# Eight weight buffers filled ahead of the ids' loads, and another order of the experts

## The chip, the cores and the metric

The kernel runs on one core of a Trainium2 chip. The metric is the time of one execution on the device, in microseconds, median of several runs. The core has TensorE (matmuls and transposes), VectorE, ScalarE, GpSimd (POOL), the queue engine SyncE (SP), and 16 DMA engines that all queues share.

## The reference

One encoder layer over 1536 tokens (a sequence of 1024 and one of 512) of width 1024, in fp32. A first half mixes tokens: a projection, a pooled part and differential attention, then an output projection and a residual. The second half is a mixture of experts, and the change lies there:

```python
pg = jax.nn.softmax((xt @ w_rg) + b_rg); g_top, g_idx = lax.top_k(pg, 1)      # 1 of 4 groups
...
e_top, e_loc = lax.top_k(pe, TOP_K)                                          # 2 of its 8 experts
...
hid = jax.nn.silu(xblk @ w_gate[e]) * (xblk @ w_up[e])                       # 1024 -> 512
return hid @ w_down[e]                                                       # 512 -> 1024
```

Each of the 32 experts has three matrices of 2 MB, 6 MB together. The layer's output is the residual plus the gated sum of two experts per token, and a last RMSNorm.

## The kernel before

Up to about 692 us of the span run projection, attention, output projection and routing. Then comes the expert stage, then a closing stage from about 1376 us that adds the last experts' rows, normalises and stores.

**Routing.** `route` finds for each token its two experts and writes token and gate into a table in memory with indirect DMAs from GpSimd (L945), one region per expert. `schedule` ranks experts 2 to 31 by their number of tokens while the first expert runs, and writes the ranking to `K["order"]`. Experts 0 and 1 (`STATIC`) are not ranked; they come first.

**Order and capacity.** `slots()` gives the sequence of positions: experts 0 and 1 as ranks 30 and 31, then the ranks in the order of the constant `ORDER`; rank 0 is the expert with the most tokens. `CAPS` gives each rank its capacity, the number of rows that are computed for it: 252, 252, 208, 200, 192, 160, 160, 160, 128, ... down to 32, and 148 and 48 for experts 0 and 1. A capacity is cut into blocks of up to 128 rows. At a capacity of 64 or less the expert is "whole": its weights are used raw, in fp32 matmuls (L1071 for w_gate and w_up, L1083 for w_down). Above that the weights are split into a high and a low part, high by ScalarE (L104), low by VectorE (L108), and a full block takes three matmuls per weight tile (L112 to L114); a block of up to 64 rows beside a full one takes two (L1113, L1114).

**The order of the work.** TensorE, VectorE, ScalarE and SP run in the written order. At position i TensorE does w_gate of i, w_up of i, then w_down of i-1. In between come transposes of the rows of i+1 and of the hidden values of i-1 (L1129), whose results ScalarE and VectorE take out of PSUM (L1138, L1139). GpSimd gathers the rows of i+2 (L1149) and adds results of i-1 to memory (L1204). SP loads the ids, which the gathers and the scatters need, four positions ahead (L1064).

**Weights.** A matrix is loaded in two pieces of 1 MB (`fetch`, L1047), numbered in the order of use: pieces 0 and 1 are w_gate of position 0, 2 and 3 w_up of 0, 4 and 5 w_gate of 1, 6 and 7 w_up of 1, 8 and 9 w_down of 0, and so on. There are `RAW` = 8 buffers, so piece k+8 waits until piece k has been split, or, for a whole expert, until its matmuls have read it. Each piece has two halves, the unit of splitting; splits are issued `AHEAD` = 7 halves ahead of the matmuls, and the split halves have `CUT` = 8 buffers.

**The start.** Pieces 0 and 1 are loaded during attention. `fetch(SOON)` loads the pieces below number SOON on SP as soon as the right-hand memory is free; behind it on SP stand the ids' loads of positions 0 and 1, which wait until routing has written the table. During the first block of expert 0 (64 rows that were known early) no further pieces are fetched. Then the pieces up to number 9 are fetched from ScalarE's queue, and from there on the splits issue them on SP:

```python
        at = [0, 0, 0, SOON]
...
        fetch(SOON)
...
        for i in range(STATIC):
            ids(i)
            gather(i)
...
        at[3] = len(stream) + 2
...
        fetch(6 * STATIC - 2, nc.scalar)
        ids(2)
```

Of the kernel before, what the change touches and what calls it, by code (L numbers as in the profile page):

```python
# [32 lines left out]
STATIC = 2  # L33
RAW, CUT = 8, 8
AHEAD = 7
SOON = 6
FIRST = 2
FINAL = (2,) * 6
LAST = (2, 3, 4, 3)
# [6 lines left out]
PACE = (3, 1, 1, 1, 1, 1, 1, 0)  # L46
WHOLE = 64
DELAY = dict(out=1, hidden=1, silu=1, evac=1, turn_h=2, turn_x=4, end_h=3, stack=3)
ORDER = (0, 17, 18, 13, 1, 19, 20, 14, 2, 21, 22, 8, 3, 23, 24, 15, 4, 27, 9, 5, 26, 16, 6, 25, 10, 12, 7, 11, 29, 28)
CAPS = (252, 252, 208, 200, 192, 160, 160, 160, 128, 112, 108, 100, 96, 88, 80, 76, 72, 64, 64, 60, 60, 56, 56, 52, 48, 36) + (32,) * 4 + (148, 48)  # L50
VORDER = tuple(range(8, 12)) + tuple(range(8))
TGORDER = (2, 0, 1)
# [1165 lines left out]
def slots():  # L1218

    return [(NE - STATIC + e, e) for e in range(STATIC)] + [(j, None) for j in ORDER]  # L1220

# [67 lines left out]
def experts(tc, A, S, K, RO, outs):  # L1289
    nc = tc.nc  # L1290
    E = Experts(tc, A, S, K)
    with ExitStack() as ctx:
# [47 lines left out]
        raws, pieces = {}, {}  # L1340
        at = [0, 0, 0, SOON]

# [21 lines left out]
        def fetch(k, queue=None):  # L1364
            while len(stream) <= at[0] < k:
                tail_step(at[0] - len(stream))
                at[0] += 1
            while at[0] < min(k, len(stream)):
                name, i, h = stream[at[0]]
                raws[at[0]] = E.fetch(name, expert(i), h, queue)  # L1370
                at[0] += 1
# [50 lines left out]
        E.open_weights(ctx, RAW - FIRST, CUT, side="right")  # L1422
        fetch(SOON)
        for _ in rest:
# [159 lines left out]
```

## Time and profile before

| | us |
|---|---|
| median of 3 runs | 1425.19 |
| lowest and highest | 1423.98, 1440.15 |
| profiled execution | 1428.79 |
| its span, first to last instruction | 1426.9 |
| TensorE busy in the span | 1312.8 |
| VectorE busy | 810.1 |
| ScalarE busy | 658.3 |

All times in the rows are microseconds from the start of the span. The granted clock of TensorE is a share of 2.4 GHz; it has two levels, 1.2 and 2.4 GHz. The DMA share is the mean busy share of the 16 DMA engines; in a short window it can be a little over 1, since a packet counts where it starts.

### The profile page before, as it was taken

The page shows a single profiled execution, that of the slowest core. Times are in us where ns is not written, and L with a number is a line of the kernel's source. Part 1 is how long each engine was busy: PE and PEld are TensorE (multiplying, and loading weights), DVE is VectorE, ACT ScalarE, POOL GpSimd, SP SyncE. Part 2 cuts the span into 40 slices and gives each one's busy share as a digit, 9 for nine tenths or more (in the row PEclk, how much of TensorE's full clock was granted, in tenths as well). Part 3 has the DMA queues.
Part 4 walks back from the last instruction along what each step waited for, and adds up shares of the span by engine and source line. Part 5 has one row for each costly group of instructions (what it writes and reads, how often), then busy time and mean ns, then how long its engine had stood idle before and what let it go on. Part 6 is the DMA issues. An engine that isn't in the chain of part 4 may idle for free.

```text
span 1426.9 us, 17476 instructions
## 1 busy us (share of the span) xinstructions
PE 1312.8 (92%) x5962; PEld 897.0 (63%) x5962; DVE 810.1 (57%) x1350; ACT 658.3 (46%) x1028; POOL 235.0 (16%) x376
## 2 busy tenths in 40 slices
PE   7999999988999999998679989999999999999980
PEld 5768888855666668776447456464655665567630
DVE  5586643066988727654734363444527566587555
ACT  6321112166887713221423453535537556577551
POOL 0000000004332210211212111121212022211233
PEclk9999999999999999999889989999999999999985
DMA  8635425436650048312488988989999998999884
GB/s 284 230 111 196 155 96 148 89 86 151 160 134 33 31 167 273 122 60 96 184 295 274 345 330 302 376 328 322 370 326 378 361 370 320 355 359 370 304 333 170
DMA packets 91621, 335.06 MB, mean 235 GB/s; under 512 B 19594, under 2 KB 27274, under 8 KB 66954
## 3 DMA queue, kind: packets, MB, share of 16 engines
q1 hardware_dynamic: 79913, 302.95, 59.0%
q0 software_dynamic: 11040, 26.78, 8.0%
q10 hardware_dynamic: 576, 4.19, 0.8%
q8 instruction: 48, 0.79, 0.2%
q14 instruction: 44, 0.35, 0.1%
HBM read 281.25 MB, written 52.62 MB: 234 GB/s over the span
## 4 chain that ended last, share of the span: by engine, by line
PE 76%; DMA 12%; DVE 5%; ACT 3%; POOL 2%; issue 1%; SPq 0%; ACTq 0%; POOLq 0%; DVEq 0%
PE pm_m L112 8%; PE pm_m L114 7%; PE pm_m L113 7%; PE pm_m L1071 6%; DMA er_raw<-w_gate 6%; PE pz_z L113 5%; PE pz_z L112 5%; PE pz_z L114 5%; PE ps_sc L393 5%; PE po_o L451 5%; PE pt_t L1129 3%; PE ph_h L113 3%; PE ph_h L114 3%; PE ph_h L112 3%; PE pm_m L1083 3%; PE pt_t L438 2%
## 5 line engine op out<-in xcount | busy, mean ns | idle before, releaser
L108 DVE TENSOR_TENSOR ew_lo<-er_raw,ew_hi 128x1024 fp32r<-128x1024 f32 x216 | 257.4, 1218 | 143.6 <-ACT ew_hi L104 143.3
L104 ACT ACTIVATE ew_hi<-er_raw 128x1024 fp32r<-128x1024 f32 x216 | 220.4, 1050 | 48.9 <-DMA er_raw<-w_gate 26.6
L112 PE MATMUL pm_m<-ew_hi,ex_x 128*128 128x512 f32 (+9 forms) x352 | 142.3, 404 | 2.3 <-ACT ex_x L1138 2.3
L114 PE MATMUL pm_m<-ew_hi,ex_x 128*128 128x512 f32 (+9 forms) x352 | 140.0, 398 | 0.5 <-DVE ex_x L1139 0.5
L113 PE MATMUL pm_m<-ew_lo,ex_x 128*128 128x512 f32 (+9 forms) x352 | 139.6, 396 | 0.0
L1204 POOL DMA_INDIRECT acc<-ex_y,ex_ix x40 | 73.6, 1839 | 345.3 <-ACT ex_y L1198 138.7
L112 PE MATMUL pz_z<-xT_hi,w_hi 128*128 128x512 f32 x288 | 115.0, 401 | 8.4 <-ACT xT_hi L153 8.4
L113 PE MATMUL pz_z<-xT_lo,w_hi 128*128 128x512 f32 x288 | 115.0, 400 | 0.0
L114 PE MATMUL pz_z<-xT_hi,w_lo 128*128 128x512 f32 x288 | 113.2, 393 | 0.0
L1071 PE MATMUL pm_m<-er_raw,ex_x 128*32 128x512 f32 (+6 forms) x448 | 103.8, 598 | 0.6 <-ACT ex_x L1134 0.6
L393 PE MATMUL ps_sc<-st_st 128*128 128x512 f32 x320 | 97.5, 445 | 7.3 <-ACT sm_e L412 5.5
L408 ACT ACTIVATE sm_e<-ps_sc,sb_m 128x1024 f32<-128x1024 f32 x64 | 70.8, 1111 | 38.7 <-PE pt_t L438 37.4
L397 DVE TENSOR_REDUCE sb_m<-ps_sc 128x1 f32<-128x1024 f32 x64 | 75.3, 1218 | 22.1 <-PE ps_sc L393 22.1
L393 PEld LDWEIGHTS ps_sc<-st_st 128*128 128x128 f32 x320 | 59.7, 194 | 42.9 <-ACT sm_e L408 12.6
L112 PEld LDWEIGHTS pm_m<-ew_hi,ex_x 128*128 128x128 f32 (+9 forms) x352 | 60.7, 172 | 35.1 <-ACT ex_x L1138 9.0
L112 PE MATMUL ph_h<-wo_woh,mx_mh 128*128 128x512 f32 x192 | 78.1, 408 | 0.0
L113 PE MATMUL ph_h<-wo_wol,mx_mh 128*128 128x512 f32 x192 | 77.7, 406 | 0.0
L114 PE MATMUL ph_h<-wo_woh,mx_ml 128*128 128x512 f32 x192 | 77.6, 404 | 0.0
L451 PE MATMUL po_o<-wT_wT,v_V 128*128 128x512 f32 x160 | 77.4, 608 | 0.0
L114 PEld LDWEIGHTS pm_m<-ew_hi,ex_x 128*128 128x128 f32 (+9 forms) x352 | 60.7, 173 | 22.4 <-DVE ex_x L1139 1.2
L113 PEld LDWEIGHTS pm_m<-ew_lo,ex_x 128*128 128x128 f32 (+9 forms) x352 | 60.7, 173 | 19.8 <-issue 0.5
L112 PE MATMUL pm_m<-ew_hi,ex_h 128*128 128x512 f32 (+10 forms) x176 | 71.2, 405 | 0.0
(289 smaller groups left out, 2380.2 us busy)
## 6 DMA issues: line engine op xcount, KB each, us to landing
er_raw<-w_gate SPq DMA_DIRECT2D x64, 1024.0 KB, 14.2
er_raw<-w_up SPq DMA_DIRECT2D x62, 1024.0 KB, 11.7
er_raw<-w_down SPq DMA_DIRECT2D x62, 1024.0 KB, 16.3
st_st<-qk SPq DMA_DIRECT2D x48, 256.0 KB, 7.0
rw_raw<-w_in SPq DMA_DIRECT2D x16, 512.0 KB, 4.8
rw_raw<-xT SPq DMA_DIRECT2D x12, 512.0 KB, 5.7
x_x<-x SPq DMA_DIRECT2D x12, 512.0 KB, 5.3
qk<-rp_h SPq DMA_DIRECT2D x24, 256.0 KB
```

The lines of the kernel that those rows point to most:

```text
L104: nc.scalar.activation(hi, raw, AF.Copy)
L108: nc.vector.tensor_tensor(lo, raw, hi.bitcast(F32), OP.subtract)
L112: nc.tensor.matmul(out, lhsT=xh, rhs=wh, start=first, stop=False)
L113: nc.tensor.matmul(out, lhsT=xh, rhs=wl, start=False, stop=False)
L114: nc.tensor.matmul(out, lhsT=xl, rhs=wh, start=False, stop=last)
L393: nc.tensor.matmul(sc[:, b], lhsT=st[:, cc, 0, q0:q0 + 128], rhs=st[:, cc, i, k0:k0 + 512], start=i == 1, stop=i == 2)
L397: nc.vector.tensor_reduce(m[:, :1], sc, axis=AX.XY, op=OP.max, negate=True)
L408: nc.scalar.activation(e, sc, AF.Exp, bias=m[:, :1], accum_out=acc)
L451: nc.tensor.matmul(self.o, lhsT=V[:, self.t0 // 128 + kt, self.h * 128:(self.h + 1) * 128], rhs=self.wT[:, kt], start=kt == 0, stop=kt == ...
L1071: self.nc.tensor.matmul(p[b.at(k)], lhsT=b.x[:, i * 2 + k], rhs=w[:, k * 512:(k + 1) * 512], start=i == 0, stop=i == 3)
L1083: self.nc.tensor.matmul(banks[0][b.at(hf)], lhsT=b.h[:, i], rhs=w[:, s], start=i == 0, stop=i == 3)
L1204: self.nc.gpsimd.indirect_dma_start(out=self.E.S["acc"], out_offset=bass.IndirectOffsetOnAxis(ap=self.ix[:self.m, 0:1], axis=0), in_=self. ...
```

## The change

Two constants. SOON goes from 6 to 8: pieces 6 and 7 (w_up of position 1) are loaded by the first `fetch(SOON)` on SP, ahead of the ids' loads of positions 0 and 1, and no longer from ScalarE's queue behind the first block. ORDER is another permutation of the same 30 ranks: rank 1 (capacity 252) moves from the fifth place to the second, so that the two largest ranked experts follow expert 1 directly, and the ranks 2, 3, 4, 5 come each somewhat earlier among the small ones. The last seven places (ranks 25, 10, 12, 7, 11, 29, 28) are the same.

```diff
-SOON = 6
+SOON = 8
...
-ORDER = (0, 17, 18, 13, 1, 19, 20, 14, 2, 21, 22, 8, 3, 23, 24, 15, 4, 27, 9, 5, 26, 16, 6, 25, 10, 12, 7, 11, 29, 28)
+ORDER = (0, 1, 17, 18, 13, 2, 19, 20, 14, 3, 21, 22, 8, 4, 23, 15, 5, 24, 9, 27, 6, 26, 16, 25, 10, 12, 7, 11, 29, 28)
```

In capacities, positions 2 onward:

```
before 252 64 64 88 252 60 60 80 208 56 56 128 200 52 48 76 192 32 112 160 32 72 160 36 108 96 160 100 32 32
after  252 252 64 64 88 208 60 60 80 200 56 56 128 192 52 76 160 48 112 32 160 32 72 36 108 96 160 100 32 32
```

## Rows read from the trace of the kernel before

**Rows 1.** The page's busy time, share of the span and instructions: TensorE.

```profile
PE 1312.8 (92%) x5962; PEld 897.0 (63%) x5962; DVE 810.1 (57%) x1350; ACT 658.3 (46%) x1028; POOL 235.0 (16%) x376
```

**Rows 2.** Windows: length, busy time (instructions) by engine, granted clock, DMA share, GB/s.

```profile
706.00:711.50 5.50, 4.69 (x21) 2.98 (x20) 4.49 (x8) 2.75 (x4) 1.37 (x2) 1.00 0.02 0
776.30:784.40 8.10, 8.10 (x42) 4.86 (x42) 1.38 (x2) 0.60 (x1) 1.32 (x2) 1.00 0.35 87
784.40:806.20 21.80, 21.80 (x104) 12.73 (x102) 7.85 (x9) 11.52 (x16) 1.44 (x1) 1.00 1.02 328
757.90:1094.50 336.60, 322.55 (x1481) 188.98 (x1479) 148.52 (x162) 159.43 (x218) 56.23 (x40) 0.97 0.94 333
1122.30:1297.30 175.00, 175.00 (x834) 109.04 (x834) 121.05 (x132) 117.50 (x156) 35.76 (x22) 1.00 0.97 348
1228.40:1237.90 9.50, 9.50 (x43) 6.58 (x41) 2.35 (x3) 2.50 (x4) 0.00 (x0) 1.00 1.02 374
1376.00:1426.90 50.90, 11.83 (x24) 6.25 (x24) 31.28 (x46) 17.27 (x28) 21.82 (x47) 0.58 0.61 229
```

**Rows 3.** The chain of waits, longest pieces of three stretches: start, duration, what.

```profile
710.90 10.05 DMA ex_xg<-hn,ex_ix
721.00 1.38 PE pt_t L1129 x8
...
781.48 3.59 PE pm_m L1083 x16
785.09 16.51 DMA er_raw<-w_gate
801.72 16.47 DMA er_raw<-w_gate
818.31 20.69 DMA er_raw<-w_gate
840.18 1.23 DVE ew_lo L108
...
907.96 17.12 DMA er_raw<-w_gate
```

**Rows 4.** Groups, 757 to 1376 us: busy, mean ns, idle before and its releasers.

```profile
L104 ACT ACTIVATE ew_hi<-er_raw 128x1024 fp32r<-128x1024 f32 x198 | 202.5, 1050 | 48.9 <-DMA er_raw<-w_gate 26.6 <-DVE ex_x L1139 6.9 <-DMA er_raw<-w_up 5.5
...
L1129 PE MATMUL pt_t<-k_ident,ex_xg 128*128 128x128 f32 (+15 forms) x216 | 27.2, 258 | 10.4 <-DVE ex_x L1139 10.4
```

**Rows 5.** Windows of TensorE alone: uses at capacities 252, 160, 72, 32; a cluster.

```profile
769.58:780.84 11.26, 11.26 (x50) 1.00 0.81 271
1228.40:1237.88 9.48, 9.48 (x42) 1.00 1.02 373
1207.65:1213.32 5.67, 5.67 (x27) 1.00 1.03 324
1188.10:1191.70 3.60, 3.60 (x19) 1.00 0.99 262
815.00:855.00 40.00, 31.92 (x129) 0.87 0.89 327
```

**Rows 6.** Timeline of ScalarE's queue at the start of the stage.

```profile
711.26 0.86 ACTq L1047 DMA_DIRECT2D er_raw<-w_up  x2
```

**Rows 7.** Timeline of SP's DMA issues: start, duration, what, count.

```profile
693.18 1.01 SPq L1047 DMA_DIRECT2D er_raw<-w_gate  x2
708.21 3.67 SPq L1064 DMA_DIRECT2D ex_ix<-tab  x5
712.13 0.97 SPq L1047 DMA_DIRECT2D er_raw<-w_gate  x2
739.61 0.34 SPq L1047 DMA_DIRECT2D er_raw<-w_up  x1
...
762.10 0.35 SPq L1047 DMA_DIRECT2D er_raw<-w_down  x1
783.38 2.05 SPq L1047 DMA_DIRECT2D er_raw<-w_gate  x2
...
807.27 2.59 SPq L1047 DMA_DIRECT2D er_raw<-w_up  x2
```

**Rows 8.** The page's DMA issues: count, median us from issue to landing.

```profile
ex_xg<-hn,ex_ix POOLq DMA_INDIRECT x30, 9.6
```

**Rows 9.** The page's costliest groups: VectorE's splits.

```profile
L108 DVE TENSOR_TENSOR ew_lo<-er_raw,ew_hi 128x1024 fp32r<-128x1024 f32 x216 | 257.4, 1218 | 143.6 <-ACT ew_hi L104 143.3
```

## The prediction

> **What bounds the kernel now.** I read the page first. TensorE is busy 92% of the span [rows 1], which says little by itself: TensorE and the DMA engines are both nearly full in the expert stage, so I cut the span into stretches. [Rows 2] are the windows to look at. Between 757.9 and 1094.5 us TensorE is busy 322.55 of 336.6 us at a mean granted clock of 0.97, with the DMA engines at 0.94; between 1122.3 and 1297.3 us it is busy all 175.0 us at full clock, and the DMA engines at 0.97. So the first half of the expert stage loses TensorE time, the second half loses none and has almost no DMA time to spare. The chain of waits [rows 3] says why: in the first half it runs through weight loads (16.51, 16.47 and 20.69 us one behind the other from 785.09, and 17.12 from 907.96), each followed by a split on ScalarE and VectorE and then by transposes. ScalarE's splits are what wait: 26.6 us for w_gate loads before them, and TensorE's transposes wait 10.4 us for VectorE behind them [rows 4]. The stage's beginning hangs on something else: the gather of expert 0's second block, issued at 710.90, is 10.05 us on the chain, and transposes start at 721.00 [rows 3].
>
> **Prices.** A use is one matrix of one expert. From four uses without idle time [rows 5]: two full blocks (capacity 200 to 252) 11.26 us, a block and a side block (160, 192) 9.48, one block (72 to 128) 5.67, raw weights (capacity up to 64) 3.60. Each expert is three uses. Positions 19 to 27 before (32, 112, 160, 32, 72, 160, 36, 108, 96), with the w_down of 18 to 26, add up to 161.2 us; they took 175.0 [rows 2], so 13.8 us for nine experts, 1.53 each, is transposes and seams. An expert has six 1 MB pieces of weights; in the busy window from 784.4 the engines move 328 GB/s [rows 2], 3.2 us a piece.
>
> **SOON.** Removed: two w_up loads on ScalarE's queue at 711.26 [rows 6]. Added: the same two on SP, right behind the w_gate pair of 693.18, ahead of the five loads of ids at 708.21 [rows 7]. Their issue, 0.5 us each, hides in SP's wait for the scatters into the table. What they gain is covered: the DMA engines are empty from 706 to 711.5 (share 0.02) [rows 2], so the stream is up to 5.5 us earlier, but the next load, at 739.61, waits for a buffer that raw matmuls of expert 1 free [rows 7], and no matmul before it waits for weights. What they may cost: the ids that today find empty engines now follow 2 MB that run until about 712 (two pieces of about 3 us from 706). Ids issued at 708.21 let the gather start at 710.90, so they need under 2.7 us now. Behind them on SP stands the w_gate pair of 712.13 [rows 7], which has 40 us; behind them on POOL the gather, and for it TensorE waits. Ends: -0.5 us (a gather's median, 9.6 [rows 8], against the 10.05 here, if fewer pieces beside it help) and +5.5 (the whole empty time is spent waiting). I take **+2**: between ends, nearest to the part of the two pieces that is left at 708.21, less what the two share. By the Trainium skill (DMA: Bandwidth & Descriptors, Queues, rings and completion order) each DMA engine consumes a ring's descriptors in ring order, which speaks against this change: the ids would wait for both pieces, the term would be about +4 and the sum below +10. No row shows ids behind weights on an otherwise quiet SP queue.
>
> **ORDER.** The capacities go with the rank, so the matmuls, splits, gathers and scatters are the same in number, and only their order moves. Before, after positions 0 and 1: 252, 64, 64, 88, 252, 60, 60, 80, 208, 56, 56, 128, 200, 52, 48, 76, 192, 32, 112, 160, ...; after: 252, 252, 64, 64, 88, 208, 60, 60, 80, 200, 56, 56, 128, 192, 52, 76, 160, 48, 112, 32, 160, 32, 72, 36, and the rest from 108 is the same. SP's load of the expert number, its ids (one load more or less at a position) and POOL's gathers move along; they are issued two to four experts ahead, and that covers them.
>
> At the pair, TensorE has 33.8 us more without a break. VectorE's 24 splits at 1218 ns [rows 9] are 29.2 us of that per expert, so the cover holds with little to spare. The loads stop instead. Today nothing is issued between 762.10 and 783.38, and the engines' share falls to 0.35 from 776.3 to 784.4 [rows 7, 2], because a piece's buffer is freed by raw matmuls of expert 1, which end at 785.07 (781.48 and 3.59) [rows 3]. After, the same eight pieces go out at 783.4 and are through by 809 (8 times 3.2), and the next one (piece 30, w_up of position 5) needs the buffer of position 4's raw w_gate. Three uses of 11.26 and its own half come first: 785.1 + 33.8 + 3 = 822. So there is a new DMA gap of 13 us, and piece 30 leaves at 822 where it left at 807.27 [rows 7].
>
> Clusters: positions 2 to 17 are 287.5 us of uses (eight raw and four one-block experts, four with two blocks, w_down one behind) and 24.5 of seams, 312.0; they took 336.6 [rows 2], so 24.6 us are lost in four clusters of two or three light experts ahead of a heavy one, 6 each. After, there are again four such clusters; the last is 52, 76 ahead of 160 in place of 52, 48, 76 ahead of 192, and the first finds full buffers as it does today. Ends: -24.6 (all are covered) and 0. I take **-4**: the shape stays, only the last cluster is milder.
>
> Late: positions 19 to 27 become 48, 112, 32, 160, 32, 72, 36, 108, 96, which is 143.6 us of uses and 13.8 of seams, 157.4 where it was 175.0: a heavy expert has left the stretch. The loads hardly shrink: at 0.97 of 175.0 the engines were busy 169.8 us. Ends: 0 if the lead in the buffers pays all; 12.4 (169.8 less 157.4). At the best pace of any row, 374 GB/s over 9.5 us [rows 2], the 60.9 MB of the stretch (348 GB/s times 175), less 0.9 for 112 rows fewer gathered and scattered, need 160.4 us, a stall of 3.0. I take **+10**, as the long row is nearer than the burst. The Trainium skill (DMA: Bandwidth & Descriptors, Specifications) puts a core's HBM limit at about 358 GB/s; by that the 60.0 MB need 167.6 us and the stall is 10, so the sum stays +8, where by the burst row it would be +1. The trace goes above that limit for 9.5 us only.
>
> The closing stage after 1376 (50.9 us [rows 2]) and all ahead of 692 are untouched. **Sum: 2 - 4 + 10 = +8** on the profiled execution's 1428.79 us (span 1426.9 and 1.9 around it), 1437. That execution is 3.6 above the median of the runs, 1425.19, so I forecast **1433 us** for the median.
>
> **Rivals.** (a) Faster: the pair's 34 us of matmuls let the loads get so far ahead that the first-half losses go. Place: ScalarE's wait for w_gate [rows 4]. It decides if the eight buffers are full at the first raw expert after the pair and the first cluster closes, where today TensorE is idle for 8.1 us of 815 to 855 and has a granted clock of 0.87 [rows 5]. Against it: the buffers are full at that point today. Price -8 (the first cluster alone) to -24.6 (all four), with the late term at 3 and SOON at 0: 1404 to 1420, likeliest 1415. (b) Slower: the DMA stream sets the end. Place: piece 30. If every piece behind it keeps today's pace, its 15 us (822 less 807) come out at the end, with SOON's 2: 1442; with SOON's 5.5, 1446. For it: a share of 0.97 late. Against it: 0.94 early, so some pace can be won back. (c) Nothing: the new gap and the milder clusters cancel, or both resources are so near full that order does not count: 1425, give or take 3.
>
> **Numbers.** Forecast (+2 to +14) 0.45, (a) 0.20, (b) 0.22, (c) 0.13. About 2% (28.5 us) either way is what a measurement can tell from no change here. (a) at its full 24.6 stays inside; (b) with SOON's 5.5 and the full late term on top (15 + 5.5 + 12.4 = 33) would pass it: faster 0.02, within 0.93, slower 0.05. The range 1419 to 1447 leaves out the better part of (a), 0.13, and the end of (b), 0.05.
>
> **What would show it.** SOON: the ids of 708.21 land later and the transposes of 721.00 start 1 to 4 us later; if they start at 721 or earlier the term is nothing. Pair: the DMA share drops for about 13 us before 822, with TensorE busy throughout. Late: TensorE, full from 1122 to 1297 today, shows idle time between about 1190 and 1320 behind ScalarE's splits that wait for weights. First half: TensorE's loss between 757.9 and the end of the fourth cluster stays near 20 us. I am wrong if that loss falls under 10, or if the late stretch still has no idle time.

## The result, and the profile after

The changed kernel takes 1444.53 us (median of 4 runs, 1441.52 to 1450.02) against 1424.59 (4 runs, 1419.70 to 1440.15): ratio 1.014, 95% interval 1.0111 to 1.0170, some 20 us slower. The forecast was 1433 within 1419 to 1447. The two profiled executions stand closer, 1443.25 to 1428.79 with spans of 1441.1 and 1426.9, as the one of before lay above its median. The traces therefore explain 14.2 us; the rest is how single executions scatter (the first of the last four scatters into the table left between 694 and 702 us in the profiles of this study).

The page's busy line after, against [rows 1]: 5.6 us more of TensorE for the same 5962 instructions.

```profile
PE 1318.4 (91%) x5962; PEld 901.6 (63%) x5962; DVE 809.9 (56%) x1350; ACT 659.4 (46%) x1028; POOL 240.5 (17%) x376
```

Windows after (columns as in [rows 2]): from position 2 to the last w_down; the late stretch (positions 19 to 27); two pieces of the late stretch; the loads' gap behind the pair; three steps of the start.

```profile
762.95:1388.21 625.26, 603.16 (x2789) 364.49 (x2787) 321.37 (x352) 330.80 (x445) 113.48 (x72) 0.98 0.93 334
1141.76:1312.04 170.28, 160.44 (x750) 93.39 (x749) 102.17 (x112) 102.82 (x138) 32.35 (x21) 0.96 0.96 353
1184.22:1198.81 14.59, 9.75 (x40) 7.21 (x38) 12.91 (x15) 11.06 (x14) 0.00 (x0) 0.77 1.02 378
1298.17:1312.04 13.87, 8.90 (x40) 6.53 (x38) 12.38 (x14) 10.13 (x13) 0.00 (x0) 0.75 0.97 358
818.50:832.50 14.00, 14.00 (x64) 8.93 (x64) 2.59 (x3) 5.87 (x9) 1.62 (x1) 1.00 0.29 58
704.10:711.00 6.90, 6.90 (x26) 4.62 (x24) 5.64 (x9) 0.59 (x1) 1.86 (x1) 0.79 0.74 269
711.00:713.70 2.70, 0.06 (x1) 0.00 (x0) 0.07 (x1) 2.51 (x3) 0.00 (x0) 1.00 0.04 1
713.70:725.50 11.80, 0.00 (x0) 0.00 (x0) 1.29 (x2) 0.00 (x0) 3.51 (x4) 0.50 0.93 307
```

Windows of the kernel before that [rows 2] don't have: the whole stage from position 2, the step between the last scatter into the table and the ids, and the w_down of position 26 (108 rows) with the transposes in it.

```profile
757.89:1373.42 615.53, 599.56 (x2789) 361.46 (x2787) 322.37 (x352) 330.55 (x445) 109.52 (x73) 0.99 0.95 339
704.90:708.20 3.30, 3.30 (x17) 2.17 (x15) 3.27 (x5) 0.60 (x1) 1.87 (x1) 1.00 0.05 11
1290.50:1297.26 6.76, 6.76 (x40) 5.11 (x38) 6.61 (x9) 5.59 (x8) 0.00 (x0) 1.00 0.88 309
```

The expert stage after position 2 takes 625.26 us in place of 615.53, and it begins 5.06 us later (762.95 for 757.89). These two make up the 14.8 by which the last w_down ends later (1388.21 for 1373.42). Inside the stage, the late stretch, which lost nothing before, now has TensorE idle for 9.8 us and a granted clock of 0.96; nearly all of it lies in two pieces, one at the w_down of position 20 (112 rows), one at the w_down of position 26 (108 rows).

The chain of waits after (start, duration, what): the start of the stage, as in [rows 3], and then the two late pieces.

```profile
704.09 6.90 DMA tab<-rc_pay,rc_idx
...
711.44 1.45 DMA ex_ix<-tab
...
713.71 11.75 DMA ex_xg<-hn,ex_ix
...
725.50 1.38 PE pt_t L1129 x8
...
1147.23 14.20 DMA er_raw<-w_down
...
1161.55 18.25 DMA er_raw<-w_down
...
1179.89 1.07 ACT ew_hi L104
...
1192.52 1.05 PE pt_t L1129 x8
...
1198.81 0.23 PE pm_m L112
...
1283.55 2.73 PE pm_m L1083 x12
...
1286.30 17.17 DMA er_raw<-w_gate
...
1303.57 1.06 ACT ew_hi L104
...
1304.66 1.23 DVE ew_lo L108
1305.89 0.61 DVE ex_x L1139
...
1306.55 1.06 PE pt_t L1129 x8
...
1308.30 0.43 PE pm_m L113
```

Read the last six from the top: a weight load lands 17 us after its issue; ScalarE has waited for it, VectorE for ScalarE; VectorE's queue also holds the copy that frees a transpose bank, so TensorE's transposes wait for that; and when TensorE starts again its matmuls take 0.43 us, where the same matmul takes 0.23 at the full clock. The piece from 1298.17 takes 13.87 us where the same w_down took 6.76 in the kernel before: 4.97 us of idle TensorE (13.87 less 8.90) and 2.1 us of matmuls at the lower level (8.90 busy for 6.76).

The two loads were held back by different things. That of 1286.30 left when TensorE's raw w_down of the 36 had ended (1283.55 and 2.73) and so had freed its buffer. That of 1161.55 left when the load of 1147.23 had landed. In the trace the loads that SP and ScalarE issue, weights and ids together, signal their landings on eight semaphores in turn, and each is issued only after the last one on its semaphore, eight before it, has landed. In the kernel before, the loads of 801.72 and 818.31 in [rows 3] left in the same way. Eight buffers are therefore not the only limit on what is under way; no run tells apart what each of the two limits costs.

ScalarE's splits (757 to 1376 us, as in [rows 4]), and SP's first load behind the pair (as in [rows 7]).

```profile
L104 ACT ACTIVATE ew_hi<-er_raw 128x1024 fp32r<-128x1024 f32 x200 | 205.0, 1051 | 39.9 <-DMA er_raw<-w_gate 17.3 <-DMA er_raw<-w_up 7.5 <-PE pm_m L114 4.8
```

```profile
829.67 3.51 SPq L1047 DMA_DIRECT2D er_raw<-w_up  x2
```

ScalarE waits less for weights (17.3 and 7.5 us, before 26.6 and 5.5) and TensorE's transposes a little more (11.7 for 10.4): the sums say little, the places do.

### The profile page after: what moved, and what is told of

Read it like the earlier page. It is cut to its first block, busy times and chain, and to the rows that moved or that the text cites. A ratio compares the mean times of both kernels' runs of the same rounds, so it can differ in the third digit from the quotient of the medians.

```text
span 1441.1 us, 17477 instructions
## 1 busy us (share of the span) xinstructions
PE 1318.4 (91%) x5962; PEld 901.6 (63%) x5962; DVE 809.9 (56%) x1350; ACT 659.4 (46%) x1028; POOL 240.5 (17%) x376
## 4 chain that ended last, share of the span: by engine, by line
PE 72%; DMA 12%; DVE 7%; ACT 3%; issue 3%; POOL 2%; SPq 0%; another core or an unknown queue 0%; ACTq 0%; POOLq 0%; DVEq 0%
PE pm_m L112 7%; PE pm_m L114 7%; PE pm_m L113 7%; PE pz_z L112 5%; PE pz_z L113 5%; PE pz_z L114 5%; PE pm_m L1071 5%; PE ps_sc L393 4%; PE po_o L451 4%; DMA er_raw<-w_gate 3%; PE pm_m L1083 3%; PE pt_t L1129 3%; PE ph_h L112 2%; PE ph_h L114 2%; PE ph_h L113 2%
## 5 line engine op out<-in xcount | busy, mean ns | idle before, releaser
L104 ACT ACTIVATE ew_hi<-er_raw 128x1024 fp32r<-128x1024 f32 x216 | 220.7, 1051 | 39.9 <-DMA er_raw<-w_gate 17.3
L1204 POOL DMA_INDIRECT acc<-ex_y,ex_ix x40 | 77.8, 1945 | 381.6 <-ACT ex_y L1198 164.0
```

The lines of the kernel that those rows point to most:

```text
L104: nc.scalar.activation(hi, raw, AF.Copy)
L1204: self.nc.gpsimd.indirect_dma_start(out=self.E.S["acc"], out_offset=bass.IndirectOffsetOnAxis(ap=self.ix[:self.m, 0:1], axis=0), in_=self. ...
```

## The experiments

Each ratio is against the kernel before, timed beside the run; "the start" is measured from the first of the last four table scatters (698.38 us in the kernel before, 697.55 after), since the routing ahead of it moves by some us between executions.

**The two constants alone.** First the buffers:

```diff
-SOON = 6
+SOON = 8
```

> SOON = 8 with the order of before. Theory (scatters): the two extra pieces share the DMA engines with the four scatters into the table, which land about 3.5 us later after routing's end, and the gather beside the weights takes up to 2 us more; the ids themselves take the same 2.7 us. Transposes of expert 0's second block start 5 us later than before, and the time is +5 us, about 1430. Rival 1 (ring): the scatters land as before and the ids, behind 2 MB on SP's ring, take 5 us in place of 2.7; also about +3 to +5. Rival 2: all of the change's 20 us come from the order, and this is +0 (1425).

Measured: ratio 1.0053 (1.0031 to 1.0075), 7.6 us. Its chain at the start:

```profile
702.88 6.62 DMA tab<-rc_pay,rc_idx
...
710.33 1.63 DMA ex_ix<-tab
...
712.06 12.14 DMA ex_xg<-hn,ex_ix
```

The ids go out 13.17 us after the first of those four scatters (696.35), where it was 9.83; the gather is issued 2.54 us behind them (2.69 before); the gather takes 12.1 us (10.1). So the eight buffers cost at the scatter's landing (6.62 us for 3.3) and at the gather, and nothing at the ids.

Then the order, with six buffers:

```diff
-ORDER = (0, 17, 18, 13, 1, 19, 20, 14, 2, ...
+ORDER = (0, 1, 17, 18, 13, 2, 19, 20, 14, ...
```

> The new ORDER with SOON = 6. Theory: the start is as before (transposes at 721 +- 1), the first half gives 3 us back, and positions 19 to 27 take about 13 us more than their matmuls need: +10 us, about 1435, with idle time of TensorE in two places between 1170 and 1300. Rival (SOON counts for nothing): +15 to +20, as in the changed kernel.

Measured: ratio 1.0083 (1.0054 to 1.0113), 11.9 us; the window of its late stretch:

```profile
1130.92:1302.15 171.23, 159.82 (x750) 92.71 (x749) 102.47 (x112) 102.58 (x138) 31.43 (x21) 0.97 0.97 354
```

The late stretch loses 11.4 us of TensorE with six buffers too. 0.53% and 0.83% add up to 1.36%, and the full change has 1.4%: within these intervals the two constants work apart from each other.

**The start.** Pieces 6 and 7 on ScalarE's queue instead, ahead of the routing's end, in the old order:

```diff
         fetch(SOON)
+        fetch(8, nc.scalar)
```

> The order of before, SOON = 6 on SP, and pieces 6 and 7 issued at the same early place from ScalarE's queue, so that no weights stand ahead of the ids on SP's ring beyond those of before. Theory (scatters): the engines are as full as with SOON = 8, the scatters land as late, +4 to +6. Rival 1 (ring): nothing is ahead of the ids, +0 to +1.

Measured: ratio 1.0007 (0.9979 to 1.0034). Here the two pieces were through early, and the routing came 3 us late:

```profile
708.05 3.32 DMA tab<-rc_pay,rc_idx
...
714.01 4.61 DMA ex_xg<-hn,ex_ix
```

With no weights moving, the scatter lands after 3.32 us; the gather, with the next weight loads issued 0.91 us behind it, needs 4.61. As a test of SP's ring against the engines this one is inconclusive, since the weights were out of the way on either theory. Of the 4.9 us won from the scatter to position 1, 1.2 were left at position 16.

The other way, four buffers:

```diff
-SOON = 6
+SOON = 4
```

> The order of before with SOON = 4: only w_gate and w_up of expert 0 are loaded ahead of the ids, w_gate of expert 1 follows on ScalarE's queue. Theory (scatters): less traffic beside the table's scatters, they land 1 to 2 us earlier than before, and transposes start at 719 to 720: -1 to -2 us, about 1423, unless the six pieces on ScalarE's queue slow the gather by as much. Rival 1 (ring): the ring was empty in before already, 0.

Measured: ratio 1.0075 (1.0043 to 1.0107), slower where a gain was expected. The gather was indeed shorter (6.2 us to the transposes), but another wait came up on ScalarE:

```profile
709.31 16.74 DMA ex_ix<-tab
726.07 0.34 ACTq L1047
...
726.45 0.46 ACT ex_x L1138
```

ScalarE's issue of its sixth weight load stood for 14 us, until a load of ids had landed 16.74 us after its issue, and the copy that the first matmuls need is behind it in ScalarE's order. The trace shows why the issue waits for ids: that load of ids is the last one before it on the same semaphore. The ids' load had no weights ahead of it in SP's queue; ScalarE's first weight load left 0.32 us before it.

The four loads on ScalarE's queue moved behind the first transposes, in the kernel before:

```diff
-        fetch(6 * STATIC - 2, nc.scalar)
         ids(2)
         for b in late[0]:
             for fill, empty in b.turn_x():
                 fill()
                 empty()
+        fetch(6 * STATIC - 2, nc.scalar)
```

> The kernel before with one step moved: the weight pieces that ScalarE's queue loads at the start of the first expert's block (four of them) are issued behind the transposes of the first gathered rows, not ahead of them. Nothing else changes. Theory A (the gather of 84 rows is slow because weights move beside it on the same DMA engines): the gather takes 5 to 6.5 us in place of 10.1, the first expert starts 4 us sooner, and the pieces are late by some 15 us, which the eight buffers only partly hide: total -4 to +2. Rival B (the gather is slow by itself, whatever moves beside it): gather stays at 10, the pieces are late all the same, total 0 to +5.

Measured: ratio 1.0017 (0.9996 to 1.0038). Chain:

```profile
713.15 4.46 DMA ex_xg<-hn,ex_ix
...
719.99 18.36 DMA er_raw<-w_down
```

Theory A's half holds (4.46 us for 10.05): the gather is slow because weights move beside it. Nothing comes of it, as the weights that it was spared are then what the matmuls wait for: from the scatter to position 2 it took 59.2 us, before 59.5.

The gather varies as much between executions with one and the same start (six buffers, ScalarE's loads in their old place). Two of the runs below, the heavy pair alone and `pairs_late`:

```profile
713.40 9.95 DMA ex_xg<-hn,ex_ix
```

```profile
706.90 4.25 DMA ex_xg<-hn,ex_ix
```

What goes with it is when ScalarE's first weight load leaves. Where that is 0.3 to 0.4 us behind the gather's issue (three profiles, the kernel before among them) the gather takes 9.95 to 10.19 us, at 0.5 to 0.7 us (four) 6.77 to 8.65, at 1.1 us (`pairs_late`) 4.25. With eight buffers the gather is issued so late that the load leaves 0.5 and 0.7 us ahead of it: 12.14 and 11.75 us. So the profile of the kernel before caught one of the slow gathers. From the first scatter to position 2 the seven profiles with six buffers and the same expert there took 54.6 to 59.6 us (mean 58.1; the kernel before 59.5), those with eight 65.1 and 65.4: some 7 us, as the medians say (7.6).

**Which part of the order.** The later part alone:

```diff
+ORDER = (0, 17, 18, 13, 1, 19, 20, 14, 2, 21, 22, 8, 3, 23, 5, 15, 4, 24, 9, 27, 6, 26, 16, 25, 10, 12, 7, 11, 29, 28)
```

> Six buffers ahead, as before; of the new order only the back part: experts in places 2 to 15 (capacities 252 64 64 88 252 60 60 80 208 56 56 128 200 52) stand as before, and from place 16 on the two 160s stand early (160 76 192) and the four light ones (48, 32, 32, 32) between the heavy, as in the changed kernel, with the last thirteen or so places unchanged. Theory A (the cost of the order is that the later half has its light experts with too little transfer left in hand): about +10 us against the kernel before, 0.4 to 0.9%, all of it after the 19th expert. Rival B (the cost is the DMA queue falling idle behind the two heavy experts that stand together): no difference, within 0.2%. Rival C (any longer distance between the heavy experts costs): a little, +3 to +5.

Measured: ratio 1.0082 (1.0053 to 1.0111), 11.7 us. That is the whole cost of the order (11.9). In its late stretch TensorE is idle for 10.2 us, in the same two pieces (from 1177 and from 1291.5) for 4.5 and 4.8:

```profile
1134.51:1305.98 171.47, 161.25 (x749) 94.51 (x749) 103.12 (x112) 103.17 (x138) 29.55 (x20) 0.96 0.97 353
```

The heavy pair with its triples alone:

```diff
+ORDER = (0, 1, 17, 18, 13, 2, 19, 20, 14, 3, 21, 22, 8, 4, 23, 24, 15, 27, 9, 5, 26, 16, 6, 25, 10, 12, 7, 11, 29, 28)
```

> Six buffers ahead, as before; the second expert of 252 directly behind the first, each next heavy expert behind its three light ones (252 252 64 64 88 208 60 60 80 200 56 56 128 192 52 48 76 32 112 160 32 72 160 ...), and the later part left as before (two of the 160s stay at its middle). Theory A: the front loses 3 to 4 us less in clusters than before, the light run 52 48 76 32 112 costs some of that back, sum -4 to +2 us (0.997 to 1.002). Rival B (the pair dries out the DMA stream, 14 us of it, and that is never made up): +10 to +14 us, 0.7 to 1.0%.

Measured: ratio 1.0028 (1.0004 to 1.0053), 4 us, between A's upper end (+2) and B's lower (+10). Its windows: the front (positions 2 to 18, the same experts as before), the gap behind the pair, and the late stretch.

```profile
760.36:1124.72 364.36, 352.25 (x1617) 212.10 (x1616) 163.79 (x179) 174.27 (x237) 65.61 (x43) 0.98 0.93 324
815.00:830.00 15.00, 15.00 (x68) 9.69 (x69) 2.64 (x3) 5.91 (x9) 1.69 (x2) 1.00 0.29 56
1124.72:1305.11 180.39, 174.88 (x815) 106.16 (x814) 119.07 (x129) 116.49 (x153) 35.41 (x22) 0.98 0.99 366
```

The gap is there, with TensorE busy all through it, and the front takes what it took before (364.36 us; 757.89 to 1122.31 is 364.42). So the gap costs nothing in the front. The late stretch, with the experts of before, takes 180.39 for 175.0, behind the light run 52, 48, 76, 32 that this order has just ahead of it. Whether a part of these 5 us is the gap come due is not told apart, and the profiled execution is the slowest of its twelve (1436.70 us, median 1430.77).

**Late weights, or order of work.** The kernel before, and the new order, without the scatters that add the experts' rows:

```diff
     def out(self, ps):
         self.weigh(ps)
-        self.scatter()
```

> The kernel before without the scatters that add each expert's rows into the accumulator (the last two experts and everything else stay; the result lacks the routed experts' rows). Some 12 of the 210 MB that move from 757 to 1376 us fall away, with about half of the 17% of the DMA engines' time that gathers and scatters take. Theory A (the stalls are weights that come late because the DMA engines are full): the first-half clusters (d4, d8, d12, d16 with what hangs on them, 34 us against an even pace) shrink to under 15, total -15 to -30 us. Rival B (the stalls come from when buffers are released and from engines that work in order; the DMA engines have time enough): the clusters keep 25 us or more, total -6 to 0.

> The same omission, with the changed kernel's order and six buffers ahead. Theory A (the later half loses since its load has no spare DMA time): the two late stalls (16 us with the slow clock behind them) go, and this kernel lies within -5 to +3 us of the old order without scatters. Rival B (buffers and in-order engines): both late stalls stay, and it lies 8 to 12 us above the old order without scatters.

The second has six buffers. Measured: 0.9888 (0.9862 to 0.9914) and 0.9896 (0.9869 to 0.9924). From position 2 to the end, the two kernels in turn, then the two late pieces of the second:

```profile
752.55:1350.38 597.83, 594.55 (x2789) 359.52 (x2787) 322.42 (x352) 330.93 (x445) 57.15 (x34) 1.00 0.88 331
```

```profile
755.84:1355.60 599.76, 594.93 (x2789) 361.12 (x2787) 321.37 (x352) 330.95 (x445) 55.34 (x33) 0.99 0.87 330
1158.66:1169.60 10.94, 8.26 (x39) 6.08 (x38) 10.04 (x12) 10.32 (x13) 2.07 (x1) 0.86 0.98 407
1269.00:1279.50 10.50, 8.55 (x40) 6.20 (x39) 10.50 (x13) 8.59 (x11) 0.00 (x0) 0.84 0.92 348
```

In the old order the stage is 17.7 us shorter and TensorE is idle for 3.3 us in place of 16.0: what it lost in the clusters was lost to weights that come late beside full DMA engines (share 0.95, now 0.88; ScalarE's wait for w_gate falls from 26.6 us to 10.7, and in the kernel before no wait of ScalarE for a scatter shows). The new order is left 1.9 us behind (with the scatters and six buffers 8.8). So far theory A. But the two late pieces did not go as A said; they shrank from 14 us to 10.9 and 10.5, where 6.8 would be no loss. The chain through the first of them in the kernel without scatters has no transfer in it:

```profile
1147.11 3.60 PE pm_m L1083 x16
...
1151.47 0.68 ACT ex_y L1193
...
1152.18 1.07 ACT ew_hi L104
...
1164.08 0.70 DVE ex_x L1139
```

TensorE ends the raw w_down of position 19 at 1150.7; only then can ScalarE copy its result, and only behind that copy stand the splits for the w_down of 20 and the w_gate of 22. They and VectorE's part take until 1164.8, and TensorE has w_gate and w_up of a 32 to do in that time, 7.7 us, and a half of the w_down, 3.9. Half of rival B holds here. The chain through the second piece does begin with a transfer, a w_up load of 16.96 us.

The same late experts in another order, two with split weights between each two light ones, with six buffers (`pairs_late`):

```diff
-(..., 15, 5, 24, 9, 27, 6, 26, 16, 25, 10, 12, 7, 11, 29, 28)
+(..., 15, 5, 24, 9, 6, 27, 16, 10, 26, 12, 7, 25, 11, 29, 28)
```

> Six buffers ahead and the changed kernel's order with the same experts in its later part, but two experts with split weights between each two light ones: 160 48 112 160 32 72 108 32 96 160 36 100 32 32 in place of 160 48 112 32 160 32 72 36 108 96 160 100 32 32. In the changed order every light one is one expert away from the next, and since w_down runs one expert behind, three uses of raw weights follow each other (11 us), while the splits reach only seven half pieces ahead. Theory A (that, with the weights' lateness on top, makes the stall at the w_down of 112): that stall, 7.6 to 8.7 us with its slow clock, goes; total -5 to -9 us against the changed order with six buffers, so +3 to +7 against the kernel before (1.002 to 1.005). Rival B (only the sum of weights against TensorE's time counts in that stretch): the loss moves elsewhere in the stretch, total within 3 us of the changed order with six buffers, so 1.007 to 1.010.

Measured: ratio 0.9976 (0.9957 to 0.9994); against the new order with six buffers that is 1.07% less, 15 us, where A said 5 to 9 and B under 3. The late stretch, then the whole later part, from position 19 to the last w_down:

```profile
1123.45:1295.35 171.90, 170.47 (x805) 103.80 (x804) 110.55 (x119) 108.26 (x144) 34.93 (x22) 1.00 0.98 359
1123.45:1358.22 234.77, 233.34 (x1109) 133.53 (x1108) 141.52 (x156) 142.04 (x193) 45.66 (x28) 1.00 0.98 361
```

The later part of the new order with six buffers, which has the same experts:

```profile
1130.92:1378.30 247.38, 235.97 (x1109) 136.94 (x1108) 141.40 (x156) 142.50 (x193) 44.59 (x28) 0.98 0.93 341
```

In the late stretch TensorE is busy for 170.47 of 171.90 us at full clock; nine positions hold a 160 there in place of the 36, so it is the later part as a whole that compares the orders: 12.6 us less for the same experts. (The profiled execution is the fastest of its thirteen, 1413.72 us to a median of 1424.06.) Both late pieces have gone, the second as well, for which A had no reason: its w_gate was late behind a buffer that TensorE's raw w_down of a 36 freed only at 1286.3. This order keeps that 36 away from the 108, too, so it does not tell the two causes apart piece by piece.

**Orders that spread the light experts.**

```diff
+ORDER = (12, 15, 16, 7, 25, 9, 6, 13, 8, 10, 3, 18, 23, 0, 19, 17, 1, 21, 22, 2, 20, 11, 4, 24, 26, 5, 27, 14, 29, 28)
```

> Six buffers ahead, and an order of its own: capacities 96 76 72 160 36 112 160 88 128 108 200 64 52 252 60 64 252 56 56 208 60 100 192 48 32 160 32 80 32 32, so that the first ten experts need more TensorE time than transfer time and no more than two experts below 66 or so stand together afterwards. Theory A (what the order costs is the running shortfall of weights against TensorE's work, held up only by eight buffers): the four clusters of before, 24.6 us, shrink to some 8 to 12 us, the later half loses no more than before: total -8 to -18 us (0.987 to 0.995). Rival B (losses come from each change between a light and a heavy expert, not from the balance): no gain, within 0.3%. Rival C (the longer light tail 192 48 32 160 32 80 32 32 costs what the front gains): 0 to +6.

Measured: 1411.79 against 1426.02 us, ratio 0.9911 (0.9875 to 0.9947): faster than both kernels, by 12.7 us than before (by the ratio). From position 2 to the end 604.78 us for 615.53:

```profile
754.16:1358.94 604.78, 593.90 (x2797) 362.00 (x2795) 323.96 (x354) 332.04 (x446) 115.99 (x75) 0.99 0.97 350
```

A second one, with single light experts in front and pairs of them later:

```diff
+ORDER = (9, 14, 15, 3, 27, 10, 8, 7, 25, 13, 12, 16, 6, 26, 11, 5, 22, 19, 1, 23, 0, 21, 18, 2, 20, 24, 4, 17, 29, 28)
```

> Six buffers ahead and a second order that spreads light and heavy: capacities 112 80 76 200 32 108 128 160 36 88 96 72 160 32 100 160 56 60 252 52 252 56 64 208 60 48 192 64 32 32. No light expert next to another in the first 13 places and pairs at most afterwards, with a heavier expert right behind each pair. Theory A (runs of light experts make the stalls, and the sooner order had none of three or more): loss against an even pace 28 to 36 us after the start, where the kernel before has 44 and the first spread order 33: total -10 to -16 us against the kernel before. Rival (the many changes between light and heavy cost each a little): -5 or less gained.

Measured: ratio 0.9957 (0.9934 to 0.9981), 6 us, short of the 10 to 16 expected. In its trace TensorE is busy for 95.0 of the first 96.05 us from position 2, and idle for 13.5 of the 511 us behind them. What holds it there no run tells.

## Why the prediction was right in its places and wrong in its sizes

**SOON, forecast +2.** This is the step that failed, in its reason and its size. I put the cost on SP's ring: ids behind 2 MB of weights. The ids need no longer than before (issue to gather 2.70 us, 2.69 before), because they never meet the weights: SP issues them only when the last scatter into the table has landed, and that scatter is what waits. It takes 6.90 us beside the weights (DMA share 0.74) and 3.3 before (0.05), and lands as the weights end: in the next 2.70 us the share is 0.04. I had counted the engines' empty 5.5 us from 706 as free room for the two pieces; the scatter was in it. With the gather 1.7 us longer the start is 5.3 us later by the chain, at the end of my range (+5.5), and 7.6 by the medians of the buffers alone, beyond it. The chain says less because the gather in the profile of before was one of the slow ones (10.05 us, 4.25 to 10.19 with six buffers); I took its 10.05 as given and allowed for no more than 0.5 us of gain from fewer weights beside it. The rule that I took from the Trainium skill (DMA: Bandwidth & Descriptors, Queues, rings and completion order), descriptors in ring order, did not come into play at the start, as no ids stood behind weights there. The same section of the Trainium skill says that a completion semaphore is written only after every earlier write of that DMA engine, across its queues. I left that out. The trace agrees with it (the landing at 710.99, the weights' share falling at 711.0; with four buffers the ids that had no weights ahead of them in SP's queue landed after 16.74 us), though engines shared by turns would look alike.

**The pair.** Right: a gap in the loads with TensorE busy (14.00 of 14.00 us, share 0.29), the next w_up at 829.67, forecast 822 and 827 with the later start. Rival (b), that its 15 us come out at the end, falls in its size: the pair alone costs 4 us by the medians, and its front takes 364.36 us, as before. Rival (a) was half right: the first cluster became milder (TensorE idle for 5.3 us, 8.1 before), but over the front as a whole the pair alone gained nothing. My check of the cover there was wrong, too: an expert has 12 splits, not 24 (the 216 of [rows 9] belong to 18 experts), 14.6 us of VectorE, so the cover was wider than I said.

**Front clusters, forecast -4.** Right. From position 2 to 19 it took 378.8 us where before took 364.4 with 17.7 us less work, so -3.3; with six buffers -5.1. The later part alone gives -5.4 too, and the pair alone nothing, so it comes from the last cluster, where a 160 has replaced the 48, as the step said.

**Late, forecast +10, ends 0 and 12.4.** Right in place (forecast idle between 1190 and 1320; found at 1184 and 1298) and a little over the upper end: 170.3 us less 157.4 is +12.9. The end was mis-sized because it came from one sum, bytes over the DMA engines' time. Two things were not in it. Each stop of TensorE of some 5 us is followed by matmuls at half speed (0.43 for 0.23 us) that cost 2 to 3 us more, 5.1 of the 14.9 us that the two pieces lost against 6.8 each at full clock. And it is not the volume but the order: with the same experts the later part takes 12.6 us less when two split ones stand between each two raw ones. With single ones between, w_down, w_gate and w_up of light experts fall next to each other, ScalarE's splits stand behind the copy of a raw w_down, and the loads are held back, in the second piece by a buffer that only a raw matmul frees, in the first by a landing. How much of the 14.9 us each of these has is not told apart. The Trainium skill's HBM share of 358 GB/s per core (DMA: Bandwidth & Descriptors, Specifications), by which I would have had 10 us, did not bind: the heavy pair's kernel moves 366 GB/s over 180 us. The trace is of one core alone, and the Trainium skill (HBM Reference, Specifications (TRN2)) says that such a core measures above the share. I could have seen it: the kernel before is above 358 GB/s not for 9.5 us only, it moves 376 GB/s over the 35.7 us from 891.8 and 378 over those from 1070.1.

**Sum.** Forecast +8: +2, -4, +10. Found in the traces: about +5.3, -3.3, +12.9, which with 0.8 less in the routing, 0.6 more from the first transposes to position 2 and 0.6 less behind the last w_down is 14.1 of the spans' 14.2. By the medians it is 20, of which the buffers alone have 7.6 (4.4 to 10.7) where I had 2, and the order alone 11.9 where I had 6. The case of no change (c) falls; the sign was that of the forecast. That 1444.5 us lies inside my range is luck: the forecast's own upper end, +14, is 1439, and the range reaches 1447 for rival (b), whose mechanism, the pair's gap coming out at the end, gave 4 us at most.

## What to carry to other kernels

An idle stretch of the DMA engines is not free room if a small transfer on the path runs through it: look what lands in it before filling it. Where weights are prefetched into a few buffers, what counts is not the mean load of a stretch but which engine frees each buffer and how many uses in a row give the helpers no time; spread the cheap items so that no three of their uses meet. Add to each stall of TensorE the slow matmuls behind it, which here cost about half as much again (5.1 us to 9.8). And compare a start with more than one profile: which of two queues issued first, by less than a microsecond, went with 5 us of it here.

## What the runs showed of the hardware that was not expected

- A gather of 84 rows takes 4.25 to 4.61 us when the next weight loads leave 0.9 us or more behind it, 9.95 to 10.19 when they leave 0.3 to 0.4 us behind it, and 11.75 to 12.14 when they leave ahead of it; a scatter into the table 3.1 to 3.6 and, beside two more weight loads, 6.6 to 6.9.
- One core's DMA engines held 366 GB/s for 180 us.
- An issue of a weight load on ScalarE stood for 14 us until an ids load had landed that had the same semaphore, and ScalarE's own work behind it with it. The ids' load, at most 1 KB, took 16.74 us beside weights; another, issued 0.55 us earlier, took under 2.
